# Row softmax on one core: three chunks laid out as 48 consecutive rows per partition, loaded in two DMAs instead of three

## The chip, the cores and the metric

The kernel runs on one core of one Trainium2 chip. The metric is the device time of one execution in microseconds, lower is better. The time before is the median of eight runs; the profile is of one execution, which has its own time.

## The reference

The input `x` is 16 x 1024 x 512 in float32, 16,384 rows of 512 numbers. Each row is turned into a softmax with temperature 0.5:

```
x_scaled = x / 0.5
x_max = np.max(x_scaled, axis=-1, keepdims=True)
exp_x = np.exp(x_scaled - x_max)
return (exp_x / np.sum(exp_x, axis=-1, keepdims=True)).astype(np.float32)
```

33.55 MB are read and 33.55 MB are written. There is no matrix product.

## The kernel before

The 16,384 rows are cut into eight chunks of 2,048 rows (chunks 0 to 7). Within a chunk, partition p of SBUF's 128 holds G = 16 consecutive rows of HBM, which is 32 KiB in one run; line 35 writes this layout as `"(c p g) d -> c p g d"`. A chunk is so 4 MiB that lie together in HBM. SBUF has six buffers of one chunk (`BUFS = 6`); chunks 6 and 7 use the buffers of chunks 0 and 1 again.

Chunks are worked on in blocks: chunk 0 in three (4, 4 and 8 rows per partition), chunks 1 to 6 whole, chunk 7 in two of 8 rows. For each block:

- `shift` (lines 68 to 78) issues the chunk's load on SP if it hasn't been issued (line 66), takes the row maximum, negated, on VectorE (line 74), and doubles it to a bias (line 78).
- `exponentials` (line 103) runs one ScalarE activation per row in place, exp(2x + bias), with the row sum as a second output.
- `scale_vector` (lines 120 and 122) takes reciprocals of the sums and multiplies 7 of 8 rows by them on VectorE.
- `scale_scalar` (line 131) scales the remaining rows on ScalarE.
- `store` (line 139) issues the chunk's 4 MiB store on ScalarE's DMA queue.

The schedule is written by hand: engines execute in the order of the program's text, and the loop at line 152 runs the exponentials of block i+1 ahead of the scaling of block i, then the maximum of block i+2, then the store of block i. So the load of a chunk is issued when the maximum of its first block is programmed, on SP, which runs ahead. Only two loads wait for a buffer: that of chunk 6 for the store of chunk 0, and that of chunk 7 for the store of chunk 1. The last row of each partition of chunk 7 is loaded by GpSimd (lines 85 to 95), released by an exponential of chunk 5.

SP issues nine loads: chunk 0 in two (4 and 12 rows), chunks 1 to 6 in one each, and 15 rows of chunk 7. ScalarE's queue issues eight stores.

The loop that sets the order is:

```
    exponentials(0, rows(0)[0])
    for i in range(n):
        if i + 1 < n:
            exponentials(i + 1, rows(i + 1)[0])
        scale_vector(i)
        scale_scalar(i)
        if i + 2 < n:
            shift(i + 2)
        store(i)
```

Of the kernel before, what the change touches and what calls it, by code (L numbers as in the profile page):

```python
# [1 line left out]

# [4 lines left out]


@with_exitstack
def kernel(  # L10
    ctx: ExitStack,
    tc: tile.TileContext,
    x: bass.AP,
    out: bass.AP,
):
    nc = tc.nc
    fp32 = mybir.dt.float32
    P = nc.NUM_PARTITIONS
    AX = mybir.AxisListType.X
    EXP = mybir.ActivationFunctionType.Exp  # L20
    COPY = mybir.ActivationFunctionType.Copy
    MAX = mybir.AluOpType.max

    D = x.shape[-1]
    xf = x.flatten_outer_dims()
    of = out.flatten_outer_dims()
    N = xf.shape[0]

    G = 16
    C = N // (P * G)
    assert C * P * G == N
    xr = xf.rearrange("(c p g) d -> c p g d", p=P, g=G)
    outr = of.rearrange("(c p g) d -> c p g d", p=P, g=G)
    WHOLE = [(0, G)]
    LOADS = [[(0, 4), (4, G)]] + [WHOLE] * 6 + [[(0, G - 1)]]
    BLOCKS = [[(0, 4), (4, 8), (8, G)]] + [WHOLE] * 6 + [[(0, 8), (8, G)]]
    STORES = [WHOLE] * 8  # L40
    BMAX = 16
    BUFS = 6

    data = ctx.enter_context(tc.tile_pool(name="data", bufs=BUFS))
    stats = ctx.enter_context(tc.tile_pool(name="stats", bufs=6))

    ctx.enter_context(tc.manual_schedule())


    warm = stats.tile([P, 1], fp32, name="warm", bufs=1)  # L50
    nc.vector.memset(warm, 0.0)  # L51
    nc.scalar.activation(out=warm, in_=warm, func=EXP)  # L52

    chunks = {}
    blocks = [(c, lo, hi) for c in range(C) for lo, hi in BLOCKS[c]]
    n = len(blocks)
    biases, sums, recips = {}, {}, {}

    def load(c):
        if c < BUFS:  # L60
            chunks[c] = data.tile([P, G, D], fp32, name="xt")
        else:
            chunks[c] = chunks[c - BUFS]
        xt = chunks[c]
        for lo, hi in LOADS[c]:
            nc.sync.dma_start(out=xt[:, lo:hi, :], in_=xr[c][:, lo:hi, :])  # L66

    def shift(i):
        c, lo, hi = blocks[i]
        if c not in chunks:  # L70
            load(c)
        b = hi - lo
        negmax = stats.tile([P, BMAX], fp32, name="negmax")
        nc.vector.tensor_reduce(  # L74
            negmax[:, 0:b], chunks[c][:, lo:hi, :], axis=AX, op=MAX, negate=True
        )
        biases[i] = stats.tile([P, BMAX], fp32, name="bias")
        nc.vector.tensor_scalar_mul(biases[i][:, 0:b], negmax[:, 0:b], 2.0)  # L78

    def load_last_row(signal):
        seen = stats.tile([P, 1], fp32, name="seen", bufs=1)
        nc.gpsimd.tensor_copy(out=seen, in_=signal)  # L87
        c = C - 1
        halves = "p (h d) -> p h d"
        to = chunks[c - BUFS][:, G - 1, :].rearrange(halves, h=2)  # L90
        of_ = xr[c][:, G - 1, :].rearrange(halves, h=2)
        for p0, p1 in ((P - 2, P), (0, P - 2)):
            nc.gpsimd.dma_start(  # L93
                out=to[p0:p1], in_=of_[p0:p1], max_dma_last_dim=2 * D
            )

    def exponentials(i, rows):
        c, lo, hi = blocks[i]
        if i not in sums:
            sums[i] = stats.tile([P, BMAX], fp32, name="sums")  # L100
        for g in rows:
            row = chunks[c][:, lo + g, :]
            nc.scalar.activation(  # L103
                out=row,
                in_=row,
                func=EXP,
                bias=biases[i][:, g : g + 1],
                scale=2.0,
                accum_out=sums[i][:, g : g + 1],
            )  # L110
            if c == BUFS - 1 and g == 10:
                load_last_row(sums[i][:, g : g + 1])


    def scale_vector(i):
        c, lo, hi = blocks[i]
        b = hi - lo
        k = b - b // 8
        recips[i] = stats.tile([P, BMAX], fp32, name="recip")
        nc.vector.reciprocal(recips[i][:, 0:b], sums[i][:, 0:b])  # L120
        rows = chunks[c][:, lo : lo + k, :]
        nc.vector.tensor_mul(  # L122
            rows, rows, recips[i][:, 0:k].unsqueeze(2).broadcast_to((P, k, D))
        )

    def scale_scalar(i):
        c, lo, hi = blocks[i]
        b = hi - lo
        for g in range(b - b // 8, b):
            row = chunks[c][:, lo + g, :]  # L130
            nc.scalar.activation(  # L131
                out=row, in_=row, func=COPY, scale=recips[i][:, g : g + 1]
            )

    def store(i):
        c, _, end = blocks[i]
        for lo, hi in STORES[c]:
            if hi == end:
                nc.scalar.dma_start(
                    out=outr[c][:, lo:hi, :], in_=chunks[c][:, lo:hi, :]  # L140
                )

    shift(0)
    shift(1)

    def rows(i):
        c, lo, hi = blocks[i]
        cut = hi - lo - (2 if c == 1 else 0)
        return range(cut), range(cut, hi - lo)
# [11 lines that stand above are left out]
            exponentials(i + 1, rows(i + 1)[1])  # L161


# [1 line left out]
_INS = ['x']  # L165
_OUTS = [((16, 1024, 512), 'float32')]


# [23 lines left out]
```

## Time and profile before

| what | value |
|---|---|
| median of 8 runs | 162.15 us (162.02 to 162.72) |
| the profiled execution, its own time | 162.05 us |
| its span, first to last instruction | 160.3 us |
| VectorE (DVE) busy | 134.6 us |
| ScalarE (ACT) busy | 102.2 us |
| HBM read and written over the span | 419 GB/s |
| loads of 4 MiB on SP: issue to landing, median | 34.9 us |
| stores of 4 MiB on ACT's queue: issue to landing, median | 22.7 us |
| first store issued, last store issued | 44.11 us, 147.50 us |

The span is shorter than the time of the execution, which includes what lies around the first and last instruction. The page prints the busy share of each engine in 40 slices of about 4 us, one digit each. The DMA row is the mean busy share of the 16 DMA engines that carry all queues of the core: q1 is SP's (loads), q10 is ScalarE's (stores), q0 is GpSimd's. The trace also holds each DMA packet with its size, queue, start and duration; a packet here is the run of one partition. The costliest groups of instructions are these:

```profile
L103 ACT ACTIVATE xt<-xt,bias 128x512 f32<-128x512 f32 x128 | 90.4, 707 | 41.5 <-DVE bias L78 40.6
L74 DVE TENSOR_REDUCE negmax<-xt 128x16 f32<-128x8192 f32 (+2 forms) x11 | 69.9, 6352 | 9.5 <-DMA xt<-in_x_dram 9.5
L122 DVE TENSOR_TENSOR xt<-xt,recip 128x7168 f32<-128x7168 f32 (+2 forms) x11 | 62.0, 5637 | 0.4
```

A line gives the source line, the engine, the operation, output and input with their shapes and the count; then the busy time and the mean in ns of one; then the idle time of the engine ahead of them and what ended most of it.

### The profile page before, as it was taken

The numbers are of one execution on the slowest core, as the hardware profiler recorded it, in microseconds if no ns is written. First come the engines' busy times: TensorE is split into PE (matmuls) and PEld (weight loads), VectorE is DVE, ScalarE is ACT, GpSimd is POOL, SyncE is SP. The second block draws the span as 40 slices with busy tenths as digits, with TensorE's granted clock in tenths as the row PEclk, the third lists the DMA queues.
The fourth block names the chain that finished last, engine by engine and source line by source line (L and its number), as shares of the span: only waits on it lengthen the run. The fifth ranks groups of instructions, "written<-read, shape, count | busy, mean of one in ns | idle before, by whom it ended". The sixth has DMA issues, their size and how long they took to land.

```text
span 160.3 us, 410 instructions
## 1 busy us (share of the span) xinstructions
DVE 134.6 (84%) x45; ACT 102.2 (64%) x273; POOL 1.9 (1%) x7
## 2 busy tenths in 40 slices
DVE  0607999999999999999999999999999999957000
ACT  3071549069989972998199909991899891690000
POOL 0000000000000000000000000030000000000000
DMA  5999999999999999999999989999999999999993
GB/s 188 466 409 499 401 393 515 401 393 493 417 393 393 401 401 499 409 393 507 409 393 491 425 385 493 392 445 439 421 445 393 482 425 401 450 450 401 442 466 139
DMA packets 2578, 67.13 MB, mean 419 GB/s; under 512 B 328, under 2 KB 328, under 8 KB 400
## 3 DMA queue, kind: packets, MB, share of 16 engines
q1 hardware_dynamic: 1296, 33.29, 49.0%
q10 hardware_dynamic: 1152, 33.55, 48.5%
q0 software_dynamic: 128, 0.26, 0.4%
q14 instruction: 2, 0.02, 0.0%
HBM read 33.55 MB, written 33.55 MB: 419 GB/s over the span
## 4 chain that ended last, share of the span: by engine, by line
DVE 75%; DMA 7%; issue 5%; ACT 3%; SPq 0%
DVE negmax L74 42%; DVE xt L122 32%; DMA xt<-in_x_dram 7%; ACT xt L103 3%; DVE bias L78 1%; DVE recip L120 1%; SPq L66 0%
## 5 line engine op out<-in xcount | busy, mean ns | idle before, releaser
L103 ACT ACTIVATE xt<-xt,bias 128x512 f32<-128x512 f32 x128 | 90.4, 707 | 41.5 <-DVE bias L78 40.6
L74 DVE TENSOR_REDUCE negmax<-xt 128x16 f32<-128x8192 f32 (+2 forms) x11 | 69.9, 6352 | 9.5 <-DMA xt<-in_x_dram 9.5
L122 DVE TENSOR_TENSOR xt<-xt,recip 128x7168 f32<-128x7168 f32 (+2 forms) x11 | 62.0, 5637 | 0.4
L103 ACT ACTIVATION_READ_ACCUMULATOR xt<-xt,bias 128x1 f32 x128 | 23.9, 187 | 0.0
L131 ACT ACTIVATE xt<-xt,recip 128x512 f32<-128x512 f32 x15 | 9.9, 706 | 0.0
L120 DVE RECIPROCAL recip<-sums 128x16 f32<-128x16 f32 (+2 forms) x11 | 2.4, 219 | 1.8 <-ACT xt L103 1.8
L78 DVE TENSOR_SCALAR bias<-negmax 128x16 f32<-128x16 f32 (+2 forms) x11 | 1.9, 173 | 0.4
L52 ACT ACT_TABLE_LOAD x1 | 1.3, 1283 | 0.7 <-PEq L176 0.7
L93 POOL DMA_DIRECT2D xt<-in_x_dram x2 | 1.5, 741 | 0.6 <-issue 0.6
L87 POOL COPY seen<-sums 128x1 f32<-128x1 f32 x1 | 0.2, 183 | 103.7 <-ACT xt L103 103.7
L51 DVE MEMSET warm<- 128x1 f32 x1 | 0.1, 59 | 0.8 <-PEq L176 0.8
L52 ACT ACTIVATE warm<-warm 128x1 f32<-128x1 f32 x1 | 0.2, 203 | 0.0
L176 POOL MEMSET const-bfloat16-1.0<- 128x1 bf16 x1 | 0.1, 96 | 0.0
L176 POOL MEMSET const-uint8-127<- 128x1 uint8 x1 | 0.1, 95 | 0.0
L176 POOL MEMSET const-float32-0.0<- 128x1 f32 x1 | 0.1, 92 | 0.2 <-issue 0.2
L176 POOL MEMSET const-float32-1.0<- 128x1 f32 x1 | 0.1, 93 | 0.0
## 6 DMA issues: line engine op xcount, KB each, us to landing
out_dram<-xt ACTq DMA_DIRECT2D x8, 4096.0 KB, 22.7
xt<-in_x_dram SPq DMA_DIRECT2D x6, 4096.0 KB, 34.9
xt<-in_x_dram SPq DMA_DIRECT2D x1, 3840.0 KB, 28.0
xt<-in_x_dram SPq DMA_DIRECT2D x1, 3072.0 KB, 11.6
xt<-in_x_dram SPq DMA_DIRECT2D x1, 1024.0 KB, 4.8
xt<-in_x_dram POOLq DMA_DIRECT2D x1, 252.0 KB, 15.1
xt<-in_x_dram POOLq DMA_DIRECT2D x1, 4.0 KB, 8.7
```

Of the source, the lines that this page charges most:

```text
L51: nc.vector.memset(warm, 0.0)
L52: nc.scalar.activation(out=warm, in_=warm, func=EXP)
L74: nc.vector.tensor_reduce(negmax[:, 0:b], chunks[c][:, lo:hi, :], axis=AX, op=MAX, negate=True)
L78: nc.vector.tensor_scalar_mul(biases[i][:, 0:b], negmax[:, 0:b], 2.0)
L87: nc.gpsimd.tensor_copy(out=seen, in_=signal)
L93: nc.gpsimd.dma_start(out=to[p0:p1], in_=of_[p0:p1], max_dma_last_dim=2 * D)
L103: nc.scalar.activation(out=row, in_=row, func=EXP, bias=biases[i][:, g : g + 1], scale=2.0, accum_out=sums[i][:, g : g + 1],)
L120: nc.vector.reciprocal(recips[i][:, 0:b], sums[i][:, 0:b])
L122: nc.vector.tensor_mul(rows, rows, recips[i][:, 0:k].unsqueeze(2).broadcast_to((P, k, D)))
L131: nc.scalar.activation(out=row, in_=row, func=COPY, scale=recips[i][:, g : g + 1])
L176: nc = _bacc.Bacc("TRN2", target_bir_lowering=False, num_devices=1)
```

## The change

Chunks 2, 3 and 4 become one group of 6,144 rows. Partition p holds 48 consecutive rows of HBM (96 KiB in one run) instead of three times 16 rows that lie 4 MiB apart. The group's tile of 48 rows per partition takes the place of three buffers; chunk 2 is rows 0 to 15 of it, chunk 3 rows 16 to 31, chunk 4 rows 32 to 47. It is loaded by two DMAs on SP, of rows 0 to 21 and of rows 22 to 47. SP so issues eight loads. Chunk 3's first six rows come with the first DMA, and its maximum is taken in two VectorE instructions, of six rows and of ten. Its bias, exponentials and scaling are as before. The three chunks are still stored by one DMA each; such a store now writes runs of 32 KiB that stand 96 KiB apart in HBM. The other chunks keep their rows, loads and stores. Rows of the group are assigned to other partitions than before.

```diff
-    xr = xf.rearrange("(c p g) d -> c p g d", p=P, g=G)
-    outr = of.rearrange("(c p g) d -> c p g d", p=P, g=G)
-    WHOLE = [(0, G)]
-    LOADS = [[(0, 4), (4, G)]] + [WHOLE] * 6 + [[(0, G - 1)]]
...
+    GROUPS = [(0,), (1,), (2, 3, 4), (5,), (6,), (7,)]
+    LOADS = [
+        [(0, 4), (4, G)],
+        [(0, G)],
+        [(0, 22), (22, 48)],
+        [(0, G)],
+        [(0, G)],
+        [(0, G - 1)],
+    ]
...
+    for k, members in enumerate(GROUPS):
+        first, m = members[0], len(members)
+        hbm = slice(first * P * G, (first + m) * P * G)
+        into = xf[hbm].rearrange("(p g) d -> p g d", p=P)
+        back = of[hbm].rearrange("(p g) d -> p g d", p=P)
+        if first < BUFS:
+            xt = data.tile([P, m * G, D], fp32, name=f"xt{k}")
+        else:
+            xt = group_of[first - BUFS][0]
+        for at, c in enumerate(members):
+            group_of[c] = (xt, into, back, k, at * G)
+            chunks[c] = xt[:, at * G : (at + 1) * G, :]
+        waiting[k] = list(LOADS[k])
...
     def load(c):
-        if c < BUFS:
-            chunks[c] = data.tile([P, G, D], fp32, name="xt")
-        else:
-            chunks[c] = chunks[c - BUFS]
-        xt = chunks[c]
-        for lo, hi in LOADS[c]:
-            nc.sync.dma_start(out=xt[:, lo:hi, :], in_=xr[c][:, lo:hi, :])
+        xt, into, _, k, at = group_of[c]
+        while waiting[k] and waiting[k][0][0] < at + G:
+            lo, hi = waiting[k].pop(0)
+            nc.sync.dma_start(out=xt[:, lo:hi, :], in_=into[:, lo:hi, :])
...
-        nc.vector.tensor_reduce(
-            negmax[:, 0:b], chunks[c][:, lo:hi, :], axis=AX, op=MAX, negate=True
-        )
+        cuts = [lo, 6, hi] if c == 3 else [lo, hi]
+        for a, z in zip(cuts, cuts[1:]):
+            nc.vector.tensor_reduce(
+                negmax[:, a - lo : z - lo],
+                chunks[c][:, a:z, :],
+                axis=AX,
+                op=MAX,
+                negate=True,
+            )
...
     def store(i):
         c, _, end = blocks[i]
-        for lo, hi in STORES[c]:
-            if hi == end:
-                nc.scalar.dma_start(
-                    out=outr[c][:, lo:hi, :], in_=chunks[c][:, lo:hi, :]
-                )
+        _, _, back, _, at = group_of[c]
+        if end == G:
+            nc.scalar.dma_start(out=back[:, at : at + G, :], in_=chunks[c])
```

More of the change, by code (lines that the diff above doesn't have):

```diff
@@ L34 @@
     assert C * P * G == N
-    xr = xf.rearrange("(c p g) d -> c p g d", p=P, g=G)
-    outr = of.rearrange("(c p g) d -> c p g d", p=P, g=G)
-    WHOLE = [(0, G)]
-    LOADS = [[(0, 4), (4, G)]] + [WHOLE] * 6 + [[(0, G - 1)]]
-    BLOCKS = [[(0, 4), (4, 8), (8, G)]] + [WHOLE] * 6 + [[(0, 8), (8, G)]]
-    STORES = [WHOLE] * 8
+    GROUPS = [(0,), (1,), (2, 3, 4), (5,), (6,), (7,)]
[7 more added lines that the diff above has]
+    ]
+    BLOCKS = [[(0, 4), (4, 8), (8, G)]] + [[(0, G)]] * 6 + [[(0, 8), (8, G)]]
     BMAX = 16
     BUFS = 6
-    data = ctx.enter_context(tc.tile_pool(name="data", bufs=BUFS))
+    data = ctx.enter_context(tc.tile_pool(name="data", bufs=1))
     stats = ctx.enter_context(tc.tile_pool(name="stats", bufs=6))
@@ L52 @@
     nc.scalar.activation(out=warm, in_=warm, func=EXP)
-    chunks = {}
+    chunks, group_of, waiting = {}, {}, {}
+    for k, members in enumerate(GROUPS):
[11 more added lines that the diff above has]
+        waiting[k] = list(LOADS[k])
     blocks = [(c, lo, hi) for c in range(C) for lo, hi in BLOCKS[c]]
@@ L59, in load @@
     def load(c):
-        if c < BUFS:
-            chunks[c] = data.tile([P, G, D], fp32, name="xt")
-        else:
-            chunks[c] = chunks[c - BUFS]
-        xt = chunks[c]
-        for lo, hi in LOADS[c]:
-            nc.sync.dma_start(out=xt[:, lo:hi, :], in_=xr[c][:, lo:hi, :])
+        xt, into, _, k, at = group_of[c]
+        while waiting[k] and waiting[k][0][0] < at + G:
+            lo, hi = waiting[k].pop(0)
+            nc.sync.dma_start(out=xt[:, lo:hi, :], in_=into[:, lo:hi, :])
     def shift(i):
         c, lo, hi = blocks[i]
-        if c not in chunks:
-            load(c)
+        load(c)
         b = hi - lo
         negmax = stats.tile([P, BMAX], fp32, name="negmax")
-        nc.vector.tensor_reduce(
-            negmax[:, 0:b], chunks[c][:, lo:hi, :], axis=AX, op=MAX, negate=True
-        )
+        cuts = [lo, 6, hi] if c == 3 else [lo, hi]
[7 more added lines that the diff above has]
+            )
         biases[i] = stats.tile([P, BMAX], fp32, name="bias")
@@ L89, in load_last_row @@
         halves = "p (h d) -> p h d"
-        to = chunks[c - BUFS][:, G - 1, :].rearrange(halves, h=2)
-        of_ = xr[c][:, G - 1, :].rearrange(halves, h=2)
+        to = chunks[c][:, G - 1, :].rearrange(halves, h=2)
+        row = group_of[c][1][:, G - 1, :].rearrange(halves, h=2)
         for p0, p1 in ((P - 2, P), (0, P - 2)):
             nc.gpsimd.dma_start(
-                out=to[p0:p1], in_=of_[p0:p1], max_dma_last_dim=2 * D
+                out=to[p0:p1], in_=row[p0:p1], max_dma_last_dim=2 * D
             )
```

## The prediction

> **What bounds the kernel now.** I read the page first: busy shares, then the 40 slices, then the DMA queues.
>
> ```profile
> DVE 134.6 (84%) x45; ACT 102.2 (64%) x273; POOL 1.9 (1%) x7
> ...
> DVE  0607999999999999999999999999999999957000
> ...
> DMA  5999999999999999999999989999999999999993
> ...
> q1 hardware_dynamic: 1296, 33.29, 49.0%
> q10 hardware_dynamic: 1152, 33.55, 48.5%
> q0 software_dynamic: 128, 0.26, 0.4%
> ```
>
> Two things run nearly without a hole. VectorE is busy from 12.8 us to 147.4 us. The 16 DMA engines are busy in every slice but the first and the last, and the three data queues add up to 97.9% of the 160.3 us span: 156.9 us per engine. The page's chain puts 75% of the span on DVE, which suggests that VectorE is the bound. I checked that with the wait list and with the busy table by stretches.
>
> ```profile
> DVE negmax L74 <- DMA xt<-in_x_dram: 9.5, 2, 4.8
> DVE recip L120 <- ACT xt L103: 1.8, 1, 1.8
> ```
>
> ```profile
> 2.00:44.00 42.00, 33.43 (x15) 22.35 (x63) 0.00 (x0) 1.00 1.01 434
> 44.00:50.00 6.00, 5.93 (x4) 5.27 (x16) 0.00 (x0) 1.00 0.96 355
> ...
> 76.00:112.00 36.00, 35.86 (x9) 25.22 (x68) 1.66 (x3) 1.00 1.01 435
> 112.00:147.50 35.50, 33.38 (x14) 26.57 (x70) 0.00 (x0) 1.00 1.00 429
> 147.50:160.30 12.80, 0.00 (x0) 0.00 (x0) 0.00 (x0) 1.00 0.81 348
> ```
>
> The columns are length, DVE, ACT, POOL, clock, DMA share, GB/s. VectorE waits for loads only twice, both before 12.8 us; afterwards loads are early. DMA moves 429 to 435 GB/s whether it only loads, loads and stores, or only stores. The one stretch below that, apart from start and end, is 44 to 50 us, where the first store joins. The last store is issued at 147.50 us. In the trace's records of single DMA packets, engines start it between 148.34 and 149.12 us, and all but one engine go straight over from the store before; the one waits 0.36 us. So the slowest engine is bound by its own 156.9 us of packets, and VectorE's end has 149.12 - 148.34 = 0.78 us of slack behind that. The end is set by total DMA work; VectorE is a close second. For a gain, the change must take work off the DMA engines or close a hole in them; for a loss, it must open a hole, or hold VectorE up by over 0.78 us.
>
> **The change, part by part.** The sum is made against the profiled run: span 160.28 us, time 162.05 us, so 1.77 us lie outside the span; the median of the eight runs is 0.10 us above that run.
>
> *Fewer, longer packets.* A packet is one partition's run: 32 KiB for 16 rows. By the packet records 8 KiB takes 309 ns, 24 KiB 912, 30 KiB 1138, 32 KiB 1213, loads and stores alike. The slope is 301 ns per 8 KiB, which leaves 1213 - 4 x 301 = 9 ns fixed. Before, chunks 2 to 4 are 3 loads x 8 packets per engine x 1213 = 29.11 us. After, 8 packets of 44 KiB (9 + 5.5 x 301 = 1664 ns) and 8 of 52 KiB (9 + 6.5 x 301 = 1966) make 29.04 us. Gain: 0.07 us. The bytes are the same. Packets over 32 KiB are not in this trace. If the chip cuts each in two, there are 32 instead of 24: 8 x 9 ns = 0.07 us lost. I take the gain, as the four sizes lie on one line; both ends are inside the measurement.
>
> *One DMA fewer* (8 on SP instead of 9). The Trainium skill's page "DMA: Bandwidth & Descriptors", in the section "Anatomy of one DMA — SWDGE (gpsimd) path", gives each DMA about 2.0 us of fixed cost beside its bytes; for the GpSimd path, but it would price one DMA fewer at about -2 us. The trace disagrees for a queue with work behind: the next load's first packet starts within some 0.01 us of the end of the last one's. Fixed latency is hidden by what is queued. By the row: 0.01 us; by the page: 160.1 us for the kernel. I take the row.
>
> *Strided stores.* Chunks 2 to 4 are now stored as 32 KiB runs every 96 KiB. The same page ("Latency and other measured facts") warns that copies slow down where the pitch between partitions is a large power of two: 207 GB/s at 512 KiB. Before, the pitch is 32 KiB. As an engine serves four neighbouring partitions in a row, parallel engines stand 128 KiB apart, after the change 384 KiB. By the page's 207 instead of 435 GB/s three stores would cost 12.6 MB x (1/207 - 1/435) = 32 us more (my estimate, an upper end). All 1024 store packets at 128 KiB apart took 1213 ns, as fast as loads, and 96 and 384 KiB are no powers of two. I take 0.
>
> *The chunk-3 maximum in two parts.* DVE reductions of 4, 8 and 16 rows take 2.285, 4.413 and 8.678 us: 0.533 per row and 0.15 per instruction. Adjacent instructions overlap by 0.08, so the second costs +0.07 us of VectorE, at most 0.15. Cover: the 0.78 us of slack above. Without that it would be paid in full.
>
> *The new waits.* The third chunk's maximum (37.40 us before) now waits for 22 rows. Those packets start where load 2's did (21.8 us on a typical engine), end 8 x 1.66 = 13.3 us later at 35.1, and land by 36, as load 2 landed 0.9 us after its slowest engine's data: 1.4 us early. The second part of chunk 3's maximum starts at 54.02 + 3.35 = 57.3 us and needs 26 rows. Their packets start at 35.1 and take 15.7 us: 50.8. Store 0 is issued at 44.11 us; before, engines ran two more load packets after the one in hand and then alternated one load, one store. That leaves at most one store in between; with the 0.84 us lost around 47 us (next) and a store packet ahead of the completion, the landing is near 53, 56 at the latest if stores cut in at once. So 0. Behind that instruction VectorE has the bias and scaling of chunk 2, ScalarE chunk 3's exponentials, the ACT queue store 2: past 57.3 + 0.7 = 58 us the end moves one for one.
>
> *The dip at 47 us.* In the packet records 30 load packets there take up to 0.64 us too long, 0.84 us summed per engine, at about the same moment (47.2 to 48.2) on all 16. No view names the cause. It comes once, as the store queue starts. The same store comes at the same time after, so I take no change; the bounds are that it vanishes (-0.84) or comes twice (+0.84).
>
> *What moves.* Long packets alternate one for one with store packets, so loads win at first: store 0 starts about 2.3 us later, lands near 70.6 instead of 68.2, and load 6, which waits for it on SP, is issued then; load 5 ends near 71 instead of 75.2. The load queue is dry for a packet or two, but store 1 (issued 58.97) is queued, so the engines stay busy. Loads 6 and 7 landed at 96.1 and 115.6 us and are needed at 103.9 and 120.5: margins of 7.8 and 4.9 us. GpSimd's last row is unaffected. POOL and ACT queues gain no instructions.
>
> Sum: -0.07 - 0.01 on DMA, +0.07 on VectorE inside its slack. Span 160.20, time 161.97; by the median, 162.15 - 0.08 = 162.1 us.
>
> **Rivals.** *Slower, a second dip.* The load queue runs dry at 71 us, and its restart stalls the engines as the store queue's start did: 161.97 + 0.84 = 162.8, by the median 162.9. For it: before, neither queue ever ran dry between start and end, so only the first start shows the price. Against it: the one engine whose store queue ran dry (148.34 us) went on with a 1.22 us packet, and GpSimd's queue started at 110 us without a stall. It decides from the point where load 6 is issued less than about 1 us ahead of load 5's end (the first load: issued 0.74, first packet 1.74). By the moves above (70.6 against 71) that point is reached, so what is open is the price of a restart. Chance 0.15.
>
> *Slower, other:* the 26 rows land after 58 us, or strided stores slow by a little; up to +0.6, about 162.6. Chance 0.10.
>
> *Faster:* the dip shrinks, because it meets fewer and longer load packets; at most -0.84, so 161.3, more likely half, 161.7. The wait list speaks neither way. With the 2 us case: chance 0.17.
>
> *The change does nothing* (long rows cut up again by the hardware): 162.2, within the forecast.
>
> **Numbers.** A measurement of this kernel can tell about 0.2% (0.32 us) from no change. Forecast 162.1, within 161.83 to 162.47: chance 0.58. Slower 0.25, faster 0.17. Its own range is 161.85 to 162.4; leaving out no more than 2 in 10 takes it to 161.6 below and 162.9 above.
>
> **What would show it.** Right: DMA shares summing to about 97.8%, span near 160.2, no DVE wait for a DMA at the second chunk-3 maximum, one dip near 47 us only, load packets of about 1.66 and 1.97 us. Wrong: a second stretch below 420 GB/s near 71 us, store packets above 1213 ns for chunks 2 to 4, a DVE wait at line 93 near 57 us, or a last store issued after 148.3 us.

## The result, and the profile after

The changed kernel takes 163.36 us (median of 13 runs, 162.09 to 164.09) against 162.15 us (35 runs, 161.96 to 162.79): a ratio of 1.0068 with a 95% interval of 1.0053 to 1.0082. It is slower by about 1.1 us, where no change was forecast and 162.9 was the end of the range. It also scatters more: 2.0 us between its fastest and slowest run, against 0.8 before.

The profiled execution of the changed kernel took 164.09 us, one of its slowest, with a span of 162.0 us. Its page, first the busy shares, the slices and the queues:

```profile
DVE 134.7 (83%) x46; ACT 102.2 (63%) x273; POOL 1.9 (1%) x7
...
DVE  0608999999999999999999999999999999964000
...
DMA  5999898989997998999999989999999999999980
...
q1 hardware_dynamic: 1152, 33.29, 48.5%
q10 hardware_dynamic: 1152, 33.55, 48.0%
q0 software_dynamic: 128, 0.26, 0.4%
q14 instruction: 2, 0.02, 0.0%
```

VectorE has 0.1 us more of work, as forecast, and one instruction more (46 for 45). The three data queues add up to 96.9% of 162.0 us, which is 157.0 us per engine: the same work as before in a longer span. So something stands idle. The wait list shows that VectorE is not what is late; it lists no wait at the cut reduction, and the last store is issued at 147.54 us instead of 147.50:

```profile
DVE negmax L93 <- DMA xt<-in_x_dram: 9.4, 2, 4.8
DVE recip L143 <- ACT xt L126: 1.8, 1, 1.8
```

The busy table by stretches of the changed kernel (columns as before: length, DVE, ACT, POOL, clock, DMA share, GB/s; a packet counts where it starts) says where the engines stand idle:

```profile
50.00:54.00 4.00, 4.00 (x2) 4.00 (x12) 0.00 (x0) 1.00 0.85 369
70.00:76.00 6.00, 6.00 (x2) 5.60 (x16) 0.00 (x0) 1.00 1.00 431
147.50:158.00 10.50, 0.00 (x0) 0.00 (x0) 0.00 (x0) 1.00 0.95 412
158.00:159.00 1.00, 0.00 (x0) 0.00 (x0) 0.00 (x0) 1.00 0.08 33
159.00:160.00 1.00, 0.00 (x0) 0.00 (x0) 0.00 (x0) 1.00 0.08 33
```

The same stretches of the kernel before:

```profile
50.00:54.00 4.00, 4.00 (x1) 4.00 (x11) 0.00 (x0) 1.00 0.93 401
70.00:76.00 6.00, 6.00 (x2) 5.55 (x16) 0.00 (x0) 1.00 0.97 421
147.50:158.00 10.50, 0.00 (x0) 0.00 (x0) 0.00 (x0) 1.00 0.98 424
158.00:159.00 1.00, 0.00 (x0) 0.00 (x0) 0.00 (x0) 1.00 0.01 0
159.00:160.00 1.00, 0.00 (x0) 0.00 (x0) 0.00 (x0) 1.00 0.00 0
```

A share of 0.08 is a single 32 KiB packet of 1.21 us that starts in that microsecond (1.21 / 16): after 158.5 us one DMA engine works on alone. There is no second dip over all engines at 70 to 76 us.

The packet records do not name their engine. I joined them end to start: the next packet begins within 5 ns of the end of the one before where an engine doesn't stall, and every engine has eight packets of each DMA of 128 partitions. Where two engines are at the same point at the same moment, the joining may exchange them. By these chains the last data end at 158.5 us or earlier on 15 engines and at 160.8 us on one; before, all 16 ended between 158.1 and 158.8. The late one lost the largest part of its time at the first store. These are its packets there (size, start, duration in us; a hole is time without a packet), with those of a common engine of the same execution and, last, those of the late engine of the kernel before:

```
late engine    load 52K 43.71 1.97 | load 52K 45.68 2.45 | store 48.13 1.21 | hole 0.55 | load 52K 49.89 2.63 | store 52.52 1.21
common engine  load 52K 44.96 1.97 | load 52K 46.92 2.82 | store 49.74 1.21 |             load 52K 50.95 1.97 | store 52.91 1.21
late, before   load 32K 45.55 1.22 | load 32K 46.77 1.75 | store 48.51 1.21 |           load 32K 49.72 1.27 | store 50.99 1.21
```

Without a stall a 52 KiB packet takes 1.97 us, one of 32 KiB 1.21. The common engine loses 0.85 us once. The late engine turns to its first store 1.6 us earlier, with less loss (0.48), and then loses 1.22 us more while the others are turning to theirs. Before, it lost 0.60 us in all. In this execution it loses another 0.87 us in the two packets that it has in hand as loads 6 and 7 are issued (0.31 in the one that starts at 69.0 us, 0.56 in that of 88.7); in the repeat (e1) it does not.

There is a second difference, outside the span. Time minus span is 1.77 us (1.72 to 1.83 in 66 runs) before, and 2.06 us (2.02 to 2.09) after. The whole is about 1.0 us of span (median 161.35 against 160.4, recorded to tenths) and 0.29 us outside it.

### The profile page after: what moved, and what is told of

It reads as the page before. It is cut to its first block, busy times and chain, and to the rows that moved or that the text cites. A ratio compares the mean times of both kernels' runs of the same rounds, so it can differ in the third digit from the quotient of the medians.

```text
span 162.0 us, 408 instructions
## 1 busy us (share of the span) xinstructions
DVE 134.7 (83%) x46; ACT 102.2 (63%) x273; POOL 1.9 (1%) x7
## 4 chain that ended last, share of the span: by engine, by line
DVE 75%; DMA 7%; issue 5%; ACT 3%; SPq 0%
DVE negmax L93 41%; DVE xt L145 31%; DMA xt<-in_x_dram 7%; ACT xt L126 3%; DVE bias L101 1%; DVE recip L143 1%; SPq L83 0%
## 5 line engine op out<-in xcount | busy, mean ns | idle before, releaser
L93 DVE TENSOR_REDUCE negmax<-xt 128x16 f32<-128x8192 f32 (+4 forms) x12 | 69.9, 5836 | 9.4 <-DMA xt<-in_x_dram 9.4
```

Of the source, the lines that this page charges most:

```text
L93: nc.vector.tensor_reduce(negmax[:, a - lo : z - lo], chunks[c][:, a:z, :], axis=AX, op=MAX, negate=True,)
```

## The experiments

Theory *late engine*: the span is set by the one engine that loses most, and what it loses depends on the first store. Rivals: the 96 KiB pitch of the stores; long packets wherever they are; VectorE's cut.

**Repeat, and parts alone.** The first run repeats the changed kernel. The others change one line of it each, or of the kernel before:

```diff
-        [(0, 22), (22, 48)],
+        [(0, 16), (16, 32), (32, 48)],     # e2
+        [(0, 22), (22, 32), (32, 48)],     # e3
```

```diff
# e4, in the kernel before
-        nc.vector.tensor_reduce(
-            negmax[:, 0:b], chunks[c][:, lo:hi, :], axis=AX, op=MAX, negate=True
-        )
+        cuts = [lo, 6, hi] if c == 3 else [lo, hi]
+        for a, z in zip(cuts, cuts[1:]):
+            nc.vector.tensor_reduce(negmax[:, a - lo : z - lo],
+                chunks[c][:, a:z, :], axis=AX, op=MAX, negate=True)
```

> The changed kernel itself once more. The profile of the change shows 15 DMA engines done by 158.5 us and one at 160.8 us; that one lost extra time on packets at 49.9, 69.0 and 88.7 us. If one late engine is what costs, this run has a ratio near 1.007 again, its time is set by how late the last engine is, and the other 15 end no later than before. If it was an accident of one profile, all 16 engines end late by the same amount.

Measured: 163.45 us, ratio 1.0062 (1.0037 to 1.0086), span 161.3 us in the profile. Again one engine is late: its last data end near 160.0, all others by 158.8. So it is no accident of one profile. The late engine cost VectorE something here, too. Of the 26-row load, 15 engines' data had landed by 55.0 us and the late one's landed at 57.41, so the second part of chunk 3's maximum started 0.17 us late. The two parts took 8.92 us together instead of 8.75 (first line: the result's profile; second: this one), and the last store was issued at 147.72 us. The wait list leaves this short wait out.

```profile
53.99 8.75 DVE L93 TENSOR_REDUCE negmax<-xt 128x6 f32<-128x3072 f32 x2
54.01 8.92 DVE L93 TENSOR_REDUCE negmax<-xt 128x6 f32<-128x3072 f32 x2
```

The spans of the changed kernel fall into two groups: in 6 of 27 runs (this one and the result's) it is 159.9 to 160.4 us, in the others 161.0 to 162.2.

> Layout of 48 rows and two-part maximum kept, but loads of 16, 16 and 16 rows: packets of 32 KiB as before, stores still strided by 96 KiB. Theory 'long packets' (52 KiB packets meet the first store and put one engine behind): ratio 1.000, last store landing within about 1 us over all engines. Theory 'layout' (strided runs in HBM hurt): ratio 1.007, one engine late as in the change.

Measured: 162.44 us, ratio 1.0019 (1.0013 to 1.0025). Neither theory's number: the span is that of before (median 160.4), but 2.06 us lie outside it.

> Loads of 22, 10 and 16 rows: 44 KiB packets remain, but they are over (35 us) before the first store starts (49 us), which meets packets of 32 KiB. Theory 'long packets meet the first store': ratio 1.000. Theory 'any packet over 32 KiB hurts', wherever it is: above 1.000, some part of 0.007. Theory 'layout': 1.007.

Measured: 162.44 us, ratio 1.0018 (1.0011 to 1.0024), median span 160.4, 2.05 us outside. Packets of 44 KiB that end before the first store cost nothing in the span.

> The kernel before with chunk 3's maximum in two parts and nothing else: VectorE gets 0.07 us longer, hidden by the 0.78 us that the last store has before its slowest engine. All theories but one: ratio 1.000. Theory 'VectorE is the bound after all': +0.07 us, 1.0004, not to be told apart from none; anything near 1.007 would show that the cut itself is the cause.

Measured: 162.34 us, ratio 1.0013 (1.0007 to 1.002), median span 160.3, and 2.04 us outside. The cut costs no span; but it costs 0.2 us of time, which my sum did not have at all.

**What lies outside the span.** e5 takes the cut out of e2; e6 adds an instruction to the kernel before that does nothing for it; e11 takes one away; e17 does so in the changed kernel.

```diff
# e5, in e2
-        cuts = [lo, 6, hi] if c == 3 else [lo, hi]
+        cuts = [lo, hi]
# e6, in the kernel before
     nc.vector.memset(warm, 0.0)
+    more = stats.tile([P, 1], fp32, name="more", bufs=1)
+    nc.vector.memset(more, 0.0)
# e11 in the kernel before, e17 in the changed one
-    nc.vector.memset(warm, 0.0)
+    nc.gpsimd.memset(warm, 0.0)
```

> 48-row layout with loads of 16, 16 and 16 rows and chunk 3's maximum in one instruction: the layout alone. So far all kernels with the two-part maximum have 2.05 us of time outside the span instead of 1.77, and the kernel with 16/16/16 loads has the span of before. Theory 'layout is free, the added VectorE instruction costs 0.28 us outside the span': ratio 1.000, 1.77 us outside. Theory 'the layout costs 0.1 to 0.2 us': 1.001.

Measured: 162.12 us, ratio 1.0001 (0.9993 to 1.0009), median span 160.3, 1.75 us outside. The layout with its strided stores is free.

> The kernel before with one more memset of one column on VectorE at the start, where VectorE waits for the first load: no time inside the span. Theory 'one VectorE instruction more costs outside the span, whatever it is': 2.05 us outside, ratio 1.0015. Theory 'it is the cut reduction or its wait': 1.77 us outside, ratio 1.000.

Measured: 162.41 us, ratio 1.0016 (1.001 to 1.0022), median span 160.4, 2.07 us outside. An added memset of 59 ns, inside a wait, costs 0.3 us of time that no row of the profile shows.

> The kernel before with its one memset of a 128x1 tile on GpSimd instead of VectorE: one VectorE instruction less. If the time outside the span goes with the number of VectorE instructions, it falls below 1.77 us (by 0.28 at most: ratio 0.998); if 1.77 to 2.05 us is a single step at the 48th, it stays at 1.77 and the ratio is 1.000.

Measured: 162.14 us, ratio 1.0005 (0.9997 to 1.0013), 1.78 us outside. So it is a step in the three counts tried, not a slope: by the pages' counts, kernels with 44 and 45 VectorE instructions have about 1.77 us, those with 46 have 2.05.

> The changed kernel with its memset of a 128x1 tile on GpSimd instead of VectorE, so that VectorE has as many instructions as in the kernel before. Theory 'the 0.28 us outside the span come with one VectorE instruction more': 1.77 us outside, span 161.3 as in the change, time about 163.1. Theory 'they come with something else of the change': 2.05 us outside.

Measured: 162.35 us (161.8 to 163.41), ratio 1.0021 (0.9999 to 1.0042), 1.79 us outside. The 0.28 us are gone with one instruction. The span falls into the two groups again (160.0 to 160.4 in 7 of 14 runs, 160.7 to 161.6 in the others); that more runs than before are in the low group was not expected.

**Which engine is late, and why.** On the late engine, and only there, each profile has a packet of 8,192 bytes on the queue "instruction", which the page lists beside the data queues. In the changed kernel it comes at 37.2 us: it takes 0.31 us itself, and the next load packet is 0.34 us too long. The engine is 0.65 us behind from there. The next one follows at 97.7 us, 139 records of ScalarE later. So I took it for the fetch of ScalarE's program, and moved it:

```diff
# e8
             sums[i] = stats.tile([P, BMAX], fp32, name="sums")
+            if c < 2:
+                nc.gpsimd.memset(sums[i], 1.0)
-        for g in rows:
+        for g in rows if c > 0 else ():
...
+            if c == 1:
+                nc.scalar.activation(out=row, in_=row, func=EXP,
+                    bias=biases[i][:, g : g + 1], scale=2.0)
+                continue
# e9: e8 and, ahead of the first exponentials,
+    for _ in range(48):
+        nc.scalar.activation(out=warm, in_=warm, func=COPY)
```

> The changed kernel, but chunk 0's exponentials are left out and chunk 1's go without row sums (both chunks are scaled by 1 then), so that ScalarE has run fewer instructions by 37 us and its 8 KiB instruction fetch, which then delays one DMA engine by 0.65 us, should come near 55 us, after the first store. Theory 'the engine that the fetch made late is the one that loses at the first store': with no late engine all 16 lose about 0.85 us alike, span about 160.3, time about 162.35. Theory 'one engine loses whatever the fetch does': span near 161.3, time about 163.4.

Measured: 162.3 us, ratio 1.0009 (1.0002 to 1.0015). This kernel leaves out chunk 0's exponentials and chunk 1's row sums, so it is not a softmax; its first store is issued at 42.80 us. The fetch moved to 63.7 us, which confirms whose program it is, and the span fell to 160.1 (160.0 to 160.3 in 17 of 21 runs), about 0.3 us below the kernel before. All 16 engines begin their first store between 47.7 and 48.1 us and lose 0.8 to 1.3 us. Outside the span lie 2.18 us; this kernel also has four memsets more on GpSimd.

> The kernel with chunk 0's exponentials and chunk 1's row sums left out, which had a span of 160.1 us, with 48 small ScalarE activations at the start in place of the 48 instructions left out (ScalarE waits there anyway). The 8 KiB instruction fetch should come back to about 37 us. Theory 'the fetch makes one DMA engine late, and that engine loses at the first store': span back to about 161.3, one engine late by 2 us or more. Theory 'the missing exponentials, or the store issued at 42.8 instead of 44.1 us, were what helped': span stays at 160.1.

Measured: 162.95 us (six runs), ratio 1.0059 (1.004 to 1.0077), median span 160.8 (160.4 to 161.3). The fetch came at 26.8 us, not 37. Half of the effect is back with it. In the profile, whose span of 160.4 us is the lowest of the six, the late engine is late, but the store reached all engines with the same number of packets left (first stores at 47.7 to 48.7 us), and it lost 1.2 us there, not 1.7. The exponentials are missing here as in e8 and the store is issued at 42.82 us, so neither was what helped; and being late is not enough for the full loss.

**Long packets, or when the store arrives?** These move the first store or the packets' ends:

```diff
# e7
-        store(i)
         if i + 1 < n:
             exponentials(i + 1, rows(i + 1)[1])
+        store(i)
# e10: store(2) after the third exponential of chunk 2 instead
+            if i == 4 and g == 2:
+                store(2)
# e12
+        [(0, 24), (24, 48)],
+        cuts = [lo, 8, hi] if c == 3 else [lo, hi]
# e13 (3) and e14 (1) in the changed kernel, e15 (3) and e16 (1) in the one before
-        cut = hi - lo - (2 if c == 1 else 0)
+        cut = hi - lo - (3 if c == 1 else 0)
```

> The changed kernel with the first store issued after chunk 1's last two exponentials, about 46.2 instead of 44.1 us: by then all 52 KiB packets are in hand or next, so the store packets meet the 32 KiB packets of chunk 5's load only. Theory 'a 52 KiB packet that follows the first store packet costs the late engine about 1.1 us': the span falls from 161.3 to about 160.3, time about 162.35 (the 0.28 us outside stay), ratio 1.0015. Theory 'long packets hurt as such, or through the phase they leave the engine in': span stays near 161.3, ratio 1.007.

Measured: 163.37 us, ratio 1.006 (1.004 to 1.008), median span 161.3. This tells nothing: the store was issued at 44.18 us, 0.1 us later than in the changed kernel, while ScalarE was still at the exponentials that stand ahead of it in the program:

```profile
44.05 0.70 ACT L126 ACTIVATE xt<-xt,bias 128x512 f32<-128x512 f32 x1
44.18 0.37 ACTq L162 DMA_DIRECT2D out_dram<-xt  x1
...
44.76 0.70 ACT L126 ACTIVATE xt<-xt,bias 128x512 f32<-128x512 f32 x1
```

It is one more repeat.

> The changed kernel with the first store issued after three exponentials of chunk 2, near 47.8 us (the attempt before moved it by 0.1 us only, as ScalarE's sequencer issues a DMA ahead of work still queued). The late engine should then have no 52 KiB packet left behind its first store packet. Theory 'the loss is in the 52 KiB packet that follows the late engine's first store packet': span about 160.3, time about 162.35. Theory 'late engine and long packets, store or not': span 161.3, time 163.4. Store 1 and load 6 come later too, which should not matter while stores are queued.

Measured: 162.89 us (six runs), ratio 1.0045 (1.0029 to 1.0061), median span 160.8 (160.3 to 161.2). The issue moved to 46.24 us only, which was enough: no 52 KiB packet follows a first store. Yet the late engine lost 1.69 us, in the one packet ahead of its store, and the others 1.3 instead of 0.8. So the loss is not bound to a packet behind the first store, nor to turning to the store ahead of the others: here the late engine turned to it last (53.25 us against 51.87 to 52.56). The theory as I had put it here falls.

> The changed kernel with two loads of 24 rows (48 KiB packets) and the maximum cut at 8 rows. Theory 'the loss grows with the packet that meets the first store': the late engine loses about as much as with 52 KiB, span 161.0 to 161.3. If packet boundaries, not sizes, decide (they move by up to 1.3 us against the store), the span can be anywhere from 160.3 on; a span of 160.3 would speak for timing.

Measured: 163.32 us (five runs), ratio 1.0075 (1.0063 to 1.0087), span 161.1 to 161.4. The late engine again turns to its store first (48.41 against 49.65 to 50.08) and loses 1.63 us.

> The changed kernel with three instead of two exponentials of chunk 1 behind the first store, so that it is issued 0.7 us earlier (43.4). At about 1 us after the issue the late engine is then in the packet of 43.7 to 45.7 us and the others in that of 43.0 to 45.0: all have the same number of packets left before their first store, and the late engine starts it last. Theory 'timing': it loses once, span about 160.3. Theory 'long packets': span 161.3 as before.

Measured: 162.79 us (five runs), ratio 1.004 (1.0024 to 1.0056), span 160.6 to 161.2, median 160.7. The store was issued at 43.53 us. The long packets are all there, and 0.6 us of the 1.0 are gone. They did not go as I expected: in the profile, at the low end of the five runs, the engines fell into two groups, with first stores near 47.8 and near 50.0 us, and both lost more than before (1.0 to 1.6 us), but the late engine did not stand out.

> The changed kernel with one exponential of chunk 1 behind the first store: issued 0.7 us later (44.8). The late engine should then be in the packet of 45.7 to 47.6 us, the others in that of 45.0 to 46.9: again the same number left. Theory 'timing': span about 160.3. Theory 'long packets': 161.3.

Measured: 162.74 us, ratio 1.004 (1.0029 to 1.0051), median span 160.7 (160.5 to 161.2). Issued at 44.87 us, the store reached the late engine behind twelve others (50.48 us; those at 49.74 to 50.11) and ahead of three (52.50 to 52.61), and it lost 1.05 us. The three lost 1.6 to 1.75 us and ended last in this profile, which is again at the low end of the runs.

> The kernel before with the first store issued 0.7 us earlier. Packets of 1.21 us: a shift of 0.7 us puts the store into another part of the packet. Theory 'timing': the span may move by some tenths either way, since with short packets the second loss was 0.05 to 0.4 us in five profiles. Theory 'long packets': span 160.35 as it is.

Measured: 162.61 us (162.09 to 163.14), ratio 1.0025 (1.0014 to 1.0036), median span 160.85, up to 161.4. Nothing but the first store's place is changed, by 0.7 us, and packets are short. This is the run that decides: the kernel before has part of the same loss within reach, 0.45 us by the medians and 1.0 in its highest runs. Its engines, too, turn to the store in two groups (47.9 to 48.3 and 49.1 to 50.2 us), and lose up to 1.5 us; the late one lost 1.08 there instead of 0.60. The issue before and in this run:

```profile
44.11 0.38 ACTq L139 DMA_DIRECT2D out_dram<-xt  x1
43.37 0.37 ACTq L139 DMA_DIRECT2D out_dram<-xt  x1
```

> The kernel before with the first store issued 0.7 us later. As for the earlier one: theory 'timing' allows some tenths, theory 'long packets' 160.35; a span near 161.3 would show that short packets can lose as much.

Measured: 162.29 us, ratio 1.0009 (0.9998 to 1.0019), median span 160.55 (160.3 to 161.1); a difference is not shown.

> The same, and the first store issued one exponential later (44.8 us), which gave a span of 160.6 us. If the two causes are separate and are all there is, about 160.6 + 1.77 = 162.4 us, ratio 1.001 to 1.002; nothing in the packets' own work (0.07 us less) would make it faster than the kernel before.

```diff
# e18: e17 and e14 together
```

Measured: 162.5 us, ratio 1.0021 (1.0014 to 1.0028); median span 160.7 and 1.77 us outside add up to it, as two separate causes would. No version here beats the kernel before.

**The late engine's losses against the span.** From the packet records of nine profiled runs I took what the late engine lost against its packets' undisturbed durations: at the first fetch (37 to 39 us), from 41 to 56 us around the first store, and later (the fetch near 97 us, and the packets it has in hand as loads 6 and 7 are issued). Losses under 0.1 us behind 56 us are left out.

| profile | 1st fetch | first store | later | sum | others, first store (median) | span | span - sum |
|---|---|---|---|---|---|---|---|
| before | 0.69 | 0.60 | 0.55 | 1.84 | 0.89 | 160.3 | 158.5 |
| e5 layout alone | 0.68 | 0.53 | 0.55 | 1.76 | 0.89 | 160.3 | 158.5 |
| e14 store 0.7 later | 0.65 | 1.05 | 0.55 | 2.25 | 1.05 | 160.5 | 158.3 |
| e13 store 0.7 earlier | 0.65 | 1.18 | 0.54 | 2.37 | 1.19 | 160.6 | 158.2 |
| e10 store 2 later | 0.65 | 1.69 | 0.54 | 2.88 | 1.31 | 161.1 | 158.2 |
| e1 repeat | 0.65 | 1.73 | 0.54 | 2.92 | 1.00 | 161.3 | 158.4 |
| e17 | 0.65 | 1.10 | 1.26 | 3.01 | 0.82 | 161.1 | 158.1 |
| e12 24/24 | 0.65 | 1.63 | 0.71 | 2.99 | 0.79 | 161.2 | 158.2 |
| after | 0.64 | 1.71 | 1.42 | 3.77 | 0.83 | 162.0 | 158.2 |

The sum runs from 1.8 to 3.8 us, and span minus sum stays between 158.1 and 158.5. What the other engines lose is not in it: where this engine ends last, the span is about 158.3 us plus what it loses. It does end last in seven of the nine. In e13 it ends level with four others (159.2 to 159.3 us) and in e14 up to 0.2 us ahead of three, which had lost 1.6 to 1.75 us at the first store, so there the sum fits although the late engine does not set the end alone. In e15 it ends last, and its sum of 2.6 leaves 158.6.

The last stretches of the busy table in the kernel that moved the fetch (e8), to be read beside the 0.08 of the changed kernel; no engine works on alone at its end:

```profile
158.00:159.00 1.00, 0.00 (x0) 0.00 (x0) 0.00 (x0) 1.00 0.01 0
159.00:160.00 1.00, 0.00 (x0) 0.00 (x0) 0.00 (x0) 1.00 0.00 0
```

And of the kernel before with only its first store earlier (e15), which has no long packets: one engine alone, as in the changed kernel.

```profile
158.00:159.00 1.00, 0.00 (x0) 0.00 (x0) 0.00 (x0) 1.00 0.08 33
159.00:160.00 1.00, 0.00 (x0) 0.00 (x0) 0.00 (x0) 1.00 0.00 0
```

## Why the prediction was wrong, point by point

*Packets.* Right. 44 and 52 KiB packets took 1665 and 1966 ns (1664 and 1966 forecast), and the busy total stayed at 157.0 us per engine. In its low group the changed kernel's span may show the small gain: 159.9 to 160.4, against 160.2 to 160.8 before.

*One DMA fewer.* Right: nothing of 2 us came of it. *Strided stores.* Right: e5 gives 1.0001, and store packets stay at 1213 ns. My upper end of 32 us was a misreading. The 207 GB/s that the Trainium skill's page "DMA: Bandwidth & Descriptors" (section "Latency and other measured facts") gives at 512 KiB is for copies between HBM tensors, counted per direction, and it stands beside 214 as the full rate of such a copy; it cannot be set against 435.

*The cut and its waits.* VectorE's 0.07 us were right (8.75 for 8.68 us) and hidden. The first landing was right (35.8 us for 36). For the second I gave 53 as likely and 56 at the latest, and VectorE needed it by 57.3: it landed on 15 engines from 54.3 us, and on the late one at 57.24. In the result's profile the wait did not come, by less than 0.1 us; in the repeat it did, with 0.17 us. That was inside the 0.78 us of slack that I had given VectorE, and the late engine set the end. Where the forecast of no wait held, it held by luck, and the 53 us were wrong for that engine.

*What moves.* Store 0 landed at 69.3 us instead of 70.6, load 6 was issued at 69.4, and the load queue did not run dry; the rival of a second dip did not happen over all engines (the late one alone lost 0.31 us there, in the result's profile), and that of late rows came only as the 0.17 us of the repeat. I had found the right neighbourhood for a slowdown (the 26-row load beside store 0) and the wrong mechanism.

*The dip at 47 us* is the step that failed in the span. I had also read it too small: its load packets are up to 0.80 us too long, not 0.64, while the mean of 0.84 us per engine is right. What failed was: "The same store comes at the same time after, so I take no change". On average that holds: the median engine lost 0.83 us after, 0.89 before. But I had said myself that the slowest engine sets the end, and then summed a mean. The packet records of before showed the one engine with holes at 37.6 and 97.0 us, 1.24 us in all. It was the last by only 0.1 us (158.79 against 158.69) because it lost 0.60 us at the first store where the others lost 0.89. After, it lost 1.71. My bounds for the dip, -0.84 and +0.84, were for all engines together; the true price, +1.1 on one, lay outside them, and I gave the second dip a chance of 0.15 where the size of this one was simply unknown.

*Time outside the span* is the other failed term: I carried 1.77 us over to the changed kernel as a constant. It became 2.06, with one VectorE instruction more. This alone, 0.18% of the time, nearly uses up the 0.2% of "no change".

Together: 1.0 us of span and 0.29 us outside make 1.3; the medians differ by 1.2.

What is shown and what is not: shown is that in the changed kernel one engine, delayed by ScalarE's instruction fetch, ends the execution (the table, and e8 against e9, which give back 0.7 us of the span), and that the span follows the moment at which the first store meets the engines' packets (e13, e14 and e15 against their parents), with short packets too. How much an engine loses at a given moment is not shown: ahead of the others it lost 1.7 us, behind them 1.1 (e17) and 1.7 (e10). The long packets matter in that they put packet ends elsewhere: in the changed kernel a packet of the late engine ends at 45.68 us, just where the store takes effect; in e17 it ended at 45.59, and the engine went last instead of first. That fits the two groups of spans in one kernel, but it is two profiles; the runs without a profile leave no packet records. Why an engine is slowed while others turn to their stores stays open; no view shows it. So does why the 46th VectorE instruction costs 0.28 us outside the span.

## What to carry to other kernels

A kernel whose DMA engines are full is as slow as its slowest engine: take the packet records apart by engine before costing a change, and ask which one ends last and why, since a mean over 16 engines hides a microsecond. When such a kernel is within tenths of two bounds, moving a transfer by half a packet can cost more than the change gains; try the neighbouring issue times of both versions before judging the change itself. And compare the time outside the span as well as the span: an instruction that is free inside can cost there.

## What the runs showed of the hardware

By the joined packets, an 8 KiB instruction fetch rode on one of the 16 data engines and put it 0.65 us behind when that engine was full (0.55 at the second fetch); the two fetches lie 124 to 145 records of ScalarE apart. When a second queue started on full engines (the store issued at 44.1 us), most engines first ran the packet in hand and two more of 52 KiB, or three more of 32 KiB. They lost 0.7 to 1.2 us there (the median engine of each profile), and then alternated packet by packet. The late engine lost 0.5 to 0.8 us where it turned to its first store 0.7 to 1.0 us ahead of the median engine (seven profiles, 32 KiB packets), and 1.6 to 1.7 us where it turned 1.3 to 1.7 us ahead (four profiles, 48 and 52 KiB). A DMA that stands in ScalarE's program behind two exponentials was issued at 44.18 us, 1.3 us ahead of the end of the second (e7). One VectorE instruction more, 46 instead of 45 by the page, went with 0.28 us more outside the span in every kernel that had it (0.41 with four GpSimd memsets added, e8 and e9).
